# Half 1's output product of a two-branch decoder layer in seven products in place of eight

## The chip, the cores and the metric

The kernel runs on one core of a Trainium2 chip. The metric is the device time of one execution in microseconds (us), the median of the runs. One execution was also profiled; the rows of its trace are quoted below. Engines: TensorE (PE, with its weight loads as PEld), VectorE (DVE), ScalarE (ACT), GpSimd (POOL) and SyncE (SP), which issues nearly all DMAs, in order.

## The reference, cut to what matters

```python
xn = rms_norm(h, norm_gain[l])
proj = xn @ w_in[l]                       # queries, keys, values, gates of both branches
...                                       # o_sb: stick-breaking attention, o_sw: sliding window
y_sb = (o_sb * jax.nn.silu(sb_z)) @ w_branch_sb[l]
y_sw = (o_sw * jax.nn.silu(sw_z)) @ w_branch_swa[l]
merged = jax.nn.sigmoid(g_sb) * y_sb + jax.nn.sigmoid(g_sw) * y_sw
h = h + merged @ w_out[l]
return rms_norm(h, final_norm_gain)[:, BLOCK:]
```

There are 2048 tokens of width 1024, in float32; `w_out` is 1024 x 1024. The change concerns `merged @ w_out`, the residual sum and the last norm, for half of the tokens.

## The kernel before, in words

Tokens are cut into four groups of 512 (`GT`), and the groups into two halves of two groups; half 0 holds groups 2 and 3, half 1 groups 0 and 1. Every float32 operand of a matmul is split into a high part and a low part (`A.copy` into the high tile, then `V.tensor_tensor(..., op=ALU.subtract)` for the low one), and a product of two operands is three matmuls: high x high, high x low, low x high. All of it is bound to an order of PE that is written out by hand (`tc.manual_schedule` for the PE engine over the whole kernel). In some stretches the orders of DVE and ACT are written by hand too, and there they run in the order of the program; elsewhere a scheduler that plans with modelled times chooses the order of DVE, ACT and of SP's DMAs. An engine works its own list in order: what waits holds all that is behind it.

The stages that matter, in order of time:

1. *Half 1's gate pairs* (`gate_pairs`, L1643, called at L1910). Eight gate columns are computed in four pairs, each by seven products of half the depth (`HK` = 4 tiles) in place of eight. The sums of weights are made in `pair_weights`, one pair ahead. The argument `along` is a generator that is advanced once per pair (L1688); for half 1 it is empty. Products take the PSUM tags g, z and t in turn, two banks each. Sums out of PSUM are made by `add` (L1661), and results go to DRAM through SP (`gate_out`, L1667, L1670). The tag `xs` (`ring_x`, four tiles of 256 KB) stands idle for most of this stage.

2. *Attention* of both kinds, and in its last stretch the operands for half 0's branch products.

3. `finish` (L426) runs for half 0, then for half 1: first the sliding-window branch by seven products (`branch_by_pairs`, L328), then the stick-breaking branch (L734 to L756): for each of 8 column tiles d and 2 groups g, 12 matmuls (`project`, L449 to L451), a gate multiplication out of PSUM (L744), a sum with the other branch (L746), and the split of `merged[d, g]` (L748, L751). The output weights of the first column half are loaded and split in the same loop (`out_weights`, L601 to L611).

4. *The output product* (L758 to L809): for each group, for each token tile t of 128 rows and each column half `ch` of 512, 24 matmuls (8 depth tiles by 3) into one bank, then a DVE sum with the x row (L802), an ACT square with a row sum (L809), and after both column halves the norm (`normed`, L764, with `rsqrt`, L130) and a DMA of the rows to `out`. After the first row tile the second column half of the output weights is loaded and split (L811). In half 1 the last row tile's second column half is computed in two pieces of 256 columns, so that the closing chain (L835 to L845) starts earlier.

Half 1's output product is the last stage of the kernel; its last matmul starts at 2054.84 us of a span of 2061.5 us. DVE and ACT are in hand-written order through half 1's branch products, up to the end of the first two row tiles of the output product (`hand.close()`, L824).

The lines are those of the profile:

Of the kernel before, what the change touches and what calls it, by code (L numbers as in the profile page):

```python
# [7 lines left out]
F32 = mybir.dt.float32  # L8
# [36 lines left out]
def f32(ap):  # L45
    return ap.bitcast(F32)
# [3 lines left out]
def tile_kernel(ctx, tc, x, xt, meta, metat, gain, w_in, w_sb, w_sw, w_out, sinks, fgain,  # L50
# [201 lines left out]
    def columns(t):  # L252
        return t.rearrange("p a b c -> p (a b c)")
# [169 lines left out]
            rest = lambda d=b + 1, z=zb, w=w[1]: close(d, z, w)  # L423
        return rest

    def finish(ringl, blk, away, blocks, ahead):  # L426
# [4 lines left out]
        def bank():  # L431
            return ps("gzt"[next(banks) % 3])
# [4 lines left out]
        def small(tag, bufs):  # L437
            return cp.tile([P, GT], F32, tag=tag, name=tag, bufs=bufs)
# [32 lines left out]
        def next_half(ga, gb):  # L471
# [120 lines left out]
            yield  # L592
            yield

        gen = [blocks]
        outputs_left, last_x = [], [None]
        hand = ExitStack()
        for half, groups in enumerate(halves):
            part, merged, wo = {}, {}, {}

            def out_weights(k, ch, later=None):  # L601
                raw = small("a", AB)
                loaded[0] = DMA(raw, w_out[0, k * P:(k + 1) * P, ch * GT:(ch + 1) * GT]).ins
                ring = ringl if k < ((0, 2), (1, 3))[half][ch] else ringr
                h, l = wo[k, ch] = ring(), ring()
                A.copy(h, raw)
                low_part = lambda: V.tensor_tensor(l, raw, f32(h), op=ALU.subtract)
# [120 lines left out]
            before(14)  # L728
            if half == 0:
                DMA(fg, fgain.to_broadcast([P, D]))  # L730
            for d in range(2):
                out_weights(d, 0)
            ws_of = {}
            for d, g in [(d, g) for ds in ([0, 1], *([d] for d in range(2, 8))) for g in groups for d in ds]:  # L734
# [9 lines left out]
                V.tensor_tensor(gt, acc, gt, op=ALU.mult)  # L744
                t = part[d, g]
                V.tensor_tensor(t, gt, t, op=ALU.add)  # L746
                mh, ml = merged[d, g] = ringl(), ringl()
                A.copy(mh, t)  # L748
                for f in after:
                    f()  # L750
                after[:] = [lambda ml=ml, t=t, mh=mh: V.tensor_tensor(ml, t, f32(mh), op=ALU.subtract)]  # L751
                if g == groups[1] and d < 6:
                    out_weights(d + 2, 0, after)
            for f in after:
                f()
            del after[:]  # L756
            side = next_half(*halves[1]) if half == 0 else iter(())
            for g in groups:  # L758
                for t0 in range(0, 4, 2):
                    res, ssq, scaled_by = {}, {}, {}  # L760
# [13 lines left out]
                                V.scalar_tensor_tensor(res[t][:, cs], res[t][:, cs], rs[:, n:n + 1], fg[:, cs], op0=ALU.mult, op1=ALU.mult)  # L774
                            DMA(out[row:row + P, :], res[t])

                    end = (half, g, t0) == (1, groups[1], 2)
                    final = (half, g, t0) == (0, groups[1], 2)
                    paired = (g, t0) in ((groups[0], 0), (groups[1], 2))
                    order = [(n, t) for n in range(2) for t in (t0, t0 + 1)]  # L780
                    for ch, t in order if paired else sorted(order, key=lambda o: o[1]):
                        cs = slice(ch * GT, (ch + 1) * GT)
                        row = g * GT + t * P
                        if ch == 0:
                            res[t] = cp.tile([P, D], F32, tag="xr", name="res", bufs=3)
                            last_x[0] = DMA(res[t], x[row:row + P, :]).ins
                        ts = slice(t * P, (t + 1) * P)
                        last = end and t == 3
                        if ch == 0:
                            ssq[t] = pair[:, t - t0]  # L790
                        sum_of = ssq[t][:, ch:ch + 1]
                        if last:
                            rf = scaled_by[ch] = small("a", AB)
                        for i, c in enumerate((slice(0, GT // 2), slice(GT // 2, GT)) if last and ch else (slice(0, GT),)):
                            acc = bank()[:, :c.stop - c.start]
                            for k in range(KT):
                                (mh, ml), (wh, wl) = merged[k, g], wo[k, ch]
                                T.matmul(acc, lhsT=mh[:, ts], rhs=wh[:, c], start=k == 0, stop=False)
                                T.matmul(acc, lhsT=mh[:, ts], rhs=wl[:, c], start=False, stop=False)
                                T.matmul(acc, lhsT=ml[:, ts], rhs=wh[:, c], start=False, stop=k == KT - 1)  # L800
                            r = res[t][:, cs][:, c]
                            V.tensor_tensor(r, acc, r, op=ALU.add)  # L802
                            if last:
                                V.tensor_tensor(rf[:, c], r, fg[:, cs][:, c], op=ALU.mult)
                            if i:
                                s2 = cp.tile([P, 1], F32, tag="rs", name="rs2", bufs=4)
                                V.tensor_scalar(s2, sum_of, 1.0 / D, s0, op0=ALU.mult, op1=ALU.add)
                                s0, sum_of = s2, cp.tile([P, 2], F32, tag="ssq", name="ssq2", bufs=4)[:, 0:1]
                            A.activation(acc, r, AF.Square, accum_out=sum_of)  # L809
# [3 lines left out]
                        if (end or final) and ch and t == t0:  # L813
# [5 lines left out]
                        if last:  # L819
                            if ch == 0:  # L820
                                s0 = cp.tile([P, 1], F32, tag="rs", name="rs2", bufs=4)
                                V.tensor_scalar(s0, ssq[t][:, 0:1], 1.0 / D, EPS, op0=ALU.mult, op1=ALU.add)
                    if half and (g, t0) == (groups[0], 0):
                        hand.close()  # L824
                    if final:
                        outputs_left.append(lambda f=normed, t=t0: f(t + 1))
                    elif not end and paired:
                        normed(t0, t0 + 1)
                        next(side, None)
                    for t in (t0, t0 + 1):  # L830
                        row = g * GT + t * P
                        if end and t == 3:
                            s1 = sum_of
                            rs, u = (cp.tile([P, 1], F32, tag="rs", name="rs2", bufs=4) for _ in range(2))
                            A.activation(rs, s1, AF.Ln, bias=s0, scale=1.0 / D)  # L835
                            A.activation(rs, rs, AF.Exp, scale=-0.5)
                            V.tensor_scalar(u, s1, 1.0 / D, s0, op0=ALU.mult, op1=ALU.add)
                            V.scalar_tensor_tensor(u, rs, rs, u, op0=ALU.mult, op1=ALU.mult)
                            V.tensor_scalar(u, u, -0.5, 1.5, op0=ALU.mult, op1=ALU.add)
                            a, b = scaled_by[0], scaled_by[1]  # L840
                            A.activation(a, a, AF.Copy, scale=rs)
                            V.tensor_scalar(b, b, rs, u, op0=ALU.mult, op1=ALU.mult)
                            DMA(out[row:row + P, GT:], b)
                            A.activation(a, a, AF.Copy, scale=u)
                            A.dma_start(out[row:row + P, :GT], a)  # L845

    fst = ExitStack()
    xp = fst.enter_context(tc.tile_pool(name="x", bufs=1, side="right"))
# [778 lines left out]
    def sums_ahead(gs_, rs, short):  # L1627
# [12 lines left out]
            V.tensor_tensor(t[:, 4 * n:4 * n + 4], ssq[:, 0], ssq[:, 1], op=ALU.add)  # L1640
        rsqrt(rs, t, tp, t=u)

    def gate_pairs(ga, gb, pairs, pool, sums_x, nxt, ordered, along, between):  # L1643

        t1, t2, t3, t4 = sums_x[:4]
# [233 lines left out]
    for half, groups in enumerate(halves):  # L1879
        gts = [lambda spec=spec: gate(*spec) for spec in specs[half]]  # L1880
        if half == 1:
            with tc.tile_pool(name="fast1", bufs=1, side="left") as bp:
# [24 lines left out]
                        V.tensor_tensor(l, t, f32(h), op=ALU.subtract)  # L1907
                    byhand.close()
                hand.close()
                gate_pairs(*groups, pairs, bp, sums_x, nxt, rest, iter(()), lambda: None)  # L1910
            mid.close()
        with tc.tile_pool(name=f"swa{half}", bufs=1, side="left") as sp:
            m = half == 0
# [136 lines left out]
            A.preload_act_table_set("natural_log_exp_and_others")  # L2050
            byhand.close()
    fst.close()
    finish(ringl, blk, away, blocks[0], ahead)
    cst.close()

_OUT = (2048, 1024)
# [45 lines left out]
```

## Time and profile before

| | us |
|---|---|
| median of 3 runs | 2061.75 (2061.37 to 2062.23) |
| the profiled execution | 2063.17 |
| its span in the trace | 2061.5 |
| PE busy, of the span | 2043.9 |
| DVE busy, of the span | 1606.2 |
| ACT busy, of the span | 1160.7 |
| half 1's output product, first matmul to the tail | 1967.60 to 2055 |
| the tail, from there to the end | 6.5 |

How to read it: the span is the profiled execution from its first to its last instruction; the execution's own time is 1.7 us longer. Times in the rows are in us from the start of the span, L12 is line 12 of the kernel, and a row of the order of time has the start, the duration, the engine, the line and operation, output <- inputs, partitions x elements, and in brackets how long the engine stood idle before it and for what. Matmuls are pipelined: a row's duration overlaps the next, and what one costs is the distance between two starts.

### The profile page before, as it was taken

What the parts mean: (1) busy time and instruction counts of PE and PEld (TensorE: products, weight loads), DVE (VectorE), ACT (ScalarE), POOL (GpSimd) and SP (SyncE); (2) the same over time, 40 slices, a digit from 0 to 9 for tenths busy, and PEclk for the clock granted to TensorE, in tenths of its full rate; (3) what the DMA queues carried; (4) which work ended last, traced back from release to release, by engine and by line L of the source; (5) the groups of instructions that cost most, each with busy time, mean ns of one, the idle gap of its engine ahead of it and who ended that gap; (6) DMA issues with size and microseconds to landing.
All of it is one profiled execution on the core that took longest, in us unless ns stands there. A gap on an engine that the chain in (4) does not pass through costs nothing.

```text
span 2061.5 us, 31117 instructions
## 1 busy us (share of the span) xinstructions
PE 2043.9 (99%) x10435; PEld 1715.8 (83%) x10435; DVE 1606.2 (78%) x2639; ACT 1160.7 (56%) x2794; POOL 313.5 (15%) x642
## 2 busy tenths in 40 slices
PE   9999999999999999999999999999999999999998
PEld 7888888888888888888888888888888888887887
DVE  7898986877778787558787299999997688778843
ACT  6677775577655343357777366667765442234222
POOL 2233444431000000003332100000110003000000
PEclk9999999999999999999999999999999999999999
DMA  9855554765478566545444643333334679876822
GB/s 333 322 192 202 186 189 171 251 203 169 124 253 301 215 225 235 197 149 179 139 168 145 200 143 108 120 111 121 106 103 139 255 239 330 279 272 208 277 85 77
DMA packets 176144, 397.77 MB, mean 193 GB/s; under 512 B 24400, under 2 KB 28880, under 8 KB 175984
## 3 DMA queue, kind: packets, MB, share of 16 engines
q1 hardware_dynamic: 175696, 395.52, 56.9%
q8 instruction: 82, 1.34, 0.3%
q14 instruction: 78, 0.64, 0.1%
q10 hardware_dynamic: 288, 0.27, 0.0%
HBM read 249.02 MB, written 144.13 MB: 191 GB/s over the span
## 4 chain that ended last, share of the span: by engine, by line
PE 87%; DVE 5%; DMA 3%; ACT 3%; issue 1%; SPq 1%; POOL 0%; DVEq 0%; ACTq 0%
PE ps_g L931 34%; PE ps_o L1443 6%; PE ps_z L1386 6%; PE ps_t L1411 6%; PE ps_z L1227 3%; PE ps_o L1283 2%; PE ps_z L931 2%; PE ps_t L1261 1%; PE ps_g L1655 1%; PE ps_g L1656 1%; PE ps_g L1657 1%; PE ps_z L1655 1%; PE ps_z L1656 1%; PE ps_z L1657 1%; PE ps_o L337 1%; PE ps_t L1655 1%
## 5 line engine op out<-in xcount | busy, mean ns | idle before, releaser
L931 PE MATMUL ps_g<-xh,wh 128*128 128x512 f32 x1088 | 442.5, 407 | 0.7 <-ACT xh L1726 0.5
L931 PE MATMUL ps_g<-xl,wh 128*128 128x512 f32 x1088 | 426.3, 392 | 0.7 <-DVE xl L1727 0.6
L931 PE MATMUL ps_g<-xh,wl 128*128 128x512 f32 x1088 | 425.8, 391 | 0.0
L1396 DVE TENSOR_TENSOR_SCAN row<-row 128x512 f32<-128x512 f32 (+4 forms) x256 | 289.0, 1129 | 35.6 <-POOL row L1391 17.8
L931 PEld LDWEIGHTS ps_g<-xh,wl 128*128 128x128 f32 x1088 | 204.3, 188 | 45.1
L1389 ACT ACTIVATE row<-ps_z 128x512 f32<-128x512 f32 (+4 forms) x352 | 175.2, 509 | 110.2 <-PE ps_z L1386 106.9
L931 PEld LDWEIGHTS ps_g<-xl,wh 128*128 128x128 f32 x1088 | 205.4, 189 | 34.5 <-DVE xl L1727 2.0
L931 PEld LDWEIGHTS ps_g<-xh,wh 128*128 128x128 f32 x1088 | 205.0, 188 | 34.6 <-ACT xh L1726 1.5
L128 DVE SCALAR_TENSOR_TENSOR wtl<-ps_t,wth 128x512 fp32r<-128x512 f32 (+1 forms) x320 | 188.5, 589 | 11.3 <-ACT wth L127 11.1
L127 ACT ACTIVATE wth<-ps_t 128x512 fp32r<-128x512 f32 (+1 forms) x320 | 171.6, 536 | 43.9 <-PE ps_t L1411 40.1
L1386 PE MATMUL ps_z<-kt,q 128*128 128x512 f32 (+4 forms) x704 | 184.2, 350 | 0.7 <-ACT row L1389 0.7
L1411 PE MATMUL ps_t<-ident,row 128*128 128x128 f32 x1088 | 172.5, 274 | 3.4 <-DVE wtl L128 3.2
L1411 PEld LDWEIGHTS ps_t<-ident,row 128*128 128x128 f32 x1088 | 132.9, 140 | 38.3 <-DVE wtl L128 8.8
L1386 PEld LDWEIGHTS ps_z<-kt,q 128*128 128x128 f32 x704 | 123.8, 188 | 24.1 <-ACT row L1389 3.1
L1443 PE MATMUL ps_o<-wth,vc 128*128 128x512 f32 (+1 forms) x320 | 135.0, 422 | 0.0
L1443 PE MATMUL ps_o<-wtl,vc 128*128 128x512 f32 (+1 forms) x320 | 116.6, 364 | 0.2 <-DVE wtl L128 0.2
L1235 ACT ACTIVATE sc<-sc,nm 128x129 f32<-128x129 f32 x256 | 100.0, 393 | 29.6 <-DVE nm L1233 28.7
L1402 POOL COPY mr<-row 128x16 f32<-128x16 f32 x128 | 32.8, 258 | 385.0 <-DVE row L1396 349.8
L1220 POOL COPY sc<-skb 128x4 f32<-128x4 f32 x64 | 17.2, 276 | 459.2 <-PE ps_g L1657 304.9
L1394 DVE TENSOR_TENSOR_SCAN row<-row,mask 128x512 f32<-128x512 f32 (+2 forms) x64 | 69.8, 1098 | 16.9 <-ACT row L1389 16.8
L1082 ACT ACTIVATE tmp<-ps_g 128x512 f32<-128x512 f32 x63 | 37.8, 600 | 77.1 <-PE ps_g L931 71.3
L1267 POOL TENSOR_SCALAR_AFFINE_SELECT pm<-ph 64x256 fp32r<-64x256 f32 x128 | 63.4, 496 | 111.9 <-ACT ph L127 107.7
(679 smaller groups left out, 4651.4 us busy)
## 6 DMA issues: line engine op xcount, KB each, us to landing
wh<-h_in_w_in SPq DMA_DIRECT2D x66, 512.0 KB, 3.9
wl<-l_in_w_in SPq DMA_DIRECT2D x66, 512.0 KB, 5.1
raw<-in_w_in SPq DMA_DIRECT2D x57, 512.0 KB, 5.4
h_in_w_in<-wh SPq DMA_DIRECT2D x50, 512.0 KB, 3.1
l_in_w_in<-wl SPq DMA_DIRECT2D x50, 512.0 KB, 4.1
q<-qd SPq DMA_DIRECT2D x128, 128.0 KB, 3.1
vc<-vd SPq DMA_DIRECT2D x48, 256.0 KB, 3.2
kd<-tmp SPq DMA_DIRECT2D x32, 256.0 KB, 3.1
```

The costliest lines, as they stand in the source:

```text
L127: A.activation(h, acc, AF.Copy, scale=scale)
L128: V.scalar_tensor_tensor(l, acc, scale, f32(h), op0=ALU.mult, op1=ALU.subtract)
L931: T.matmul(acc, lhsT=a[:, k, :], rhs=b[:, k, :], start=k == i == 0, stop=k == KT - 1 and i == 2)
L1235: A.activation(sc[:, hh, :], sc[:, hh, :], AF.Exp, bias=nm[:, hh:hh + 1], accum_out=den[:, hh:hh + 1])
L1267: G.affine_select(out=pm[to, :, c], in_=full[r, :, c], pattern=[[0, 4], [sign, HB]], compare_op=ALU.is_ge, fill=0.0, base=n - 1, channel_m ...
L1386: T.matmul(z[:, :m], lhsT=qt[:, j * P:(j + 1) * P], rhs=kt[h][:, k0 + c:k0 + c + m], start=t == 0, stop=t == 1)
L1389: A.activation(r[:, c:c + m], z[:, :m], AF.Sigmoid, scale=-1.0)
L1394: V.tensor_tensor_scan(r[:, :w], r[:, :w], mask[:, :w], 1.0, op0=ALU.mult, op1=ALU.max)
L1396: V.tensor_tensor_scan(r[:, :w], r[:, :w], r[:, :w], last[j] if n else 1.0, op0=ALU.mult, op1=ALU.min)
L1411: T.transpose(tr[:, j * P:(j + 1) * P], rows_of[h, g, n - (j > i), j][:, k0:k0 + P], ident)
L1443: T.matmul(o[:, :n], lhsT=v, rhs=r, start=first and r is wh, stop=last)
L1655: T.matmul(acc, lhsT=wh[:, k, :], rhs=h[:, k, :], start=k == 0, stop=False)
```

## The change

Write merged (transposed) of half 1 as blocks by depth half and token group, and `w_out` as blocks by depth half and column half. The product of the two 2 x 2 block matrices is made by seven block products in place of eight: two token groups by two column halves. One block product has four token tiles, each of 4 depth tiles x 3 matmuls = 12 matmuls.

- `output_weight_sums` (new) is the generator that `gate_pairs` of half 1 gets as `along`. Per pair it loads four 128 x 512 tiles of `w_out`, makes four DVE sums of them in place and stores them in DRAM under the names t1 to t4.
- In `finish`, half 1's stick-breaking loop takes the column tiles in the order 0, 4, 1, 5, 2, 6, 3, 7, loads the output weights of the first column half in the order 4 to 7, 0 to 3, puts the split parts into tiles that the branch products have left (`dead`), and splits `merged` of the second group only for d >= 4. At (6, first group) it asks for four x row tiles, after the loop for the other eight pieces.
- `by_quads` (new) makes the output product. A list `todo` of 52 items (a sum or a low part on DVE, most with a copy on ACT) is worked off three at a time behind each row (`work()`). The sums of the output weights come back from DRAM (`fetched`) into tiles whose last product is over. The seven products are: second block of the first group by weight block 21; first by 11; s1 by t1; s2 by t2; s4 by block 22; s3 by t3; block 22 by t4. The products with s2, s3 and t4 accumulate in the banks of the second product (tags o and t), the one with s4 in those of the third (tags g and z). Rows are normed one behind the other (`norm`, `normed`); rows of the second group are scaled in part by ACT. The last row of the last product is computed in two pieces of 256 columns.
- The loop at L758 serves half 0 alone. DVE and ACT stay in hand-written order to the end.

The diff, cut to its core:

```diff
+        def by_quads(ga, gb, raws, a11, a12, a22, b11, b21, res, gone):
...
+            c11, c12, c21, c22 = ([raws[d, g] for d in ds] for ds, g in (
+                (range(HK), ga), (range(HK, KT), ga), (range(HK), gb), (range(HK, KT), gb)))
...
+            own("s1", osb_tiles)
+            fetched("t1", osb_tiles, weight_sums("t1"))
+            own("s2", extra)
...
+            todo = [summed(c22[k], c21[k], c22[k], ALU.add, ("s1", k)) for k in ks]
+            todo += [low_of("s1", k, c22[k], "t1") for k in ks]
+            todo += [summed(c21[k], c11[k], c21[k], ALU.subtract) for k in ks]
+            todo += [low_there("t1", k) for k in ks]
+            todo += [summed(c11[k], c22[k], c11[k], ALU.subtract, ("s2", k)) for k in ks]
+            todo += [low_of("s2", k, c11[k], "t2") for k in ks]
+            todo += [low_there("t2", k) for k in ks]
+            todo += [summed(c12[k], c12[k], c11[k], ALU.subtract, ("s4", k)) for k in ks]
+            todo += [both(low_of("s4", k, c12[k]), lambda k=k: A.copy(places["b22"][k][0], c22[k])) for k in ks]
+            todo += [low_of("b22", k, c22[k]) for k in ks]
...
+            todo += [s3_low(k) for k in ks]
+            todo += [low_there("t3", k, "t4") for k in ks]
+            todo += [low_there("t4", k) for k in ks]
+
+            def work(n=3):
+                for f in todo[:n]:
+                    f()
+                del todo[:n]
+
+            zs_ = [ps("o"), ps("t"), ps("o"), ps("t")]
+            xs_ = [ps("g"), ps("z"), ps("g"), ps("z")]
+
+            def product(acc, a, b, t, start=False, stop=False, c=slice(0, GT)):
+                ts = slice(t * P, (t + 1) * P)
+                for k in range(HK):
+                    (ah, al), (bh, bl) = a[k], b[k]
+                    T.matmul(acc[:, c], lhsT=ah[:, ts], rhs=bh[:, c], start=start and k == 0, stop=False, skip_group_check=True)
+                    T.matmul(acc[:, c], lhsT=ah[:, ts], rhs=bl[:, c], start=False, stop=False, skip_group_check=True)
+                    T.matmul(acc[:, c], lhsT=al[:, ts], rhs=bh[:, c], start=False, stop=stop and k == HK - 1, skip_group_check=True)
...
+            for t in rows:
+                product(xs_[t], a12, b21, t, True, True)
+                add(ga, t, 0, xs_[t])
+                work()
+            again = lend(*a12, *b21)
+            fetched("t2", again, weight_sums("t2"))
+            own("b22", again)
+            for t in rows:
+                product(zs_[t], a11, b11, t, True)
+                add(ga, t, 0, zs_[t])
+                work()
...
+            for k in ks:
+                DMA(c22[k], w_out[0, (k + HK) * P:(k + HK + 1) * P, GT:])
+            fetched("t3", again, weight_sums("t3"))
+            for t in rows:
+                product(xs_[t], places["s1"], places["t1"], t, True)
+                add(gb, t, 1, xs_[t])
+                work()
+            own("s3", lend(*places["s1"]))
+            fetched("t4", lend(*places["t1"]), weight_sums("t4"))
+            for t in rows:
+                product(zs_[t], places["s2"], places["t2"], t)
+                add(ga, t, 1, zs_[t])
+                work()
+            lag = []
+            for t in rows:
+                product(xs_[t], places["s4"], places["b22"], t, stop=True)
+                add(ga, t, 1, xs_[t])
+                square(ga, t, 1)
+                work()
+                lag = normed(lag, ga, t)
...
+            def seventh(t, lag):
+                product(zs_[t], places["s3"], places["t3"], t)
+                add(gb, t, 1, zs_[t])
+                square(gb, t, 1)
+                lag = normed(lag)
...
+            def fourth(t, lag):
+                product(zs_[t], a22, places["t4"], t, stop=True)
+                add(gb, t, 0, zs_[t])
+                square(gb, t, 0)
+                V.tensor_tensor(c12[t], res[gb, t][0], fg[:, :GT], op=ALU.mult)
+                return normed(lag, gb, t)
+
+            lag = seventh(0, lag)
+            lag = seventh(1, lag)
+            for t in range(3):
+                lag = fourth(t, lag)
+                if t < 2:
+                    lag = seventh(t + 2, lag)
...
+            for acc, c in zip(xs_, parts):
+                product(acc, a22, places["t4"], t, True, True, c)
+                V.tensor_tensor(r[:, c], acc[:, c], r[:, c], op=ALU.add)
+                A.activation(waste[:, c], r[:, c], AF.Square, accum_out=sum_of)
+                if c is parts[0]:
+                    normed(lag)
...
+            for c in parts:
+                V.tensor_tensor(rf[0][:, c], r[:, c], fg[:, c], op=ALU.mult)
...
+    def output_weight_sums():
+
+        for k in range(HK):
+            b11, b12, b22, b21 = (ring_x() for _ in range(4))
+            for t, (kk, ch) in ((b11, (k, 0)), (b12, (k, 1)), (b22, (k + HK, 1)), (b21, (k + HK, 0))):
+                DMA(t, w_out[0, kk * P:(kk + 1) * P, ch * GT:(ch + 1) * GT])
+            V.tensor_tensor(b11, b12, b11, op=ALU.subtract)
+            V.tensor_tensor(b12, b22, b12, op=ALU.subtract)
+            V.tensor_tensor(b22, b22, b11, op=ALU.subtract)
+            V.tensor_tensor(b21, b21, b22, op=ALU.subtract)
+            for name, t in (("t1", b11), ("t2", b22), ("t3", b12), ("t4", b21)):
+                out_sums[name, k] = dram(f"o{name}{k}", [P, GT])
+                DMA(out_sums[name, k], t)
+            yield
...
-                gate_pairs(*groups, pairs, bp, sums_x, nxt, rest, iter(()), lambda: None)
+                gate_pairs(*groups, pairs, bp, sums_x, nxt, rest, output_weight_sums(), lambda: None)
```

More of the change, by code (lines that the diff above doesn't have):

```diff
@@ L730, in finish @@
                 DMA(fg, fgain.to_broadcast([P, D]))
[L731 to L734, printed above, removed]
+            if half:
+                names = "t2", "b22", "t3", "t4"
+                first = [columns(vm[:, 2:4]), columns(vm[:, 0:2]), wm[1], wm[0]]
+                dead = iter([*(t for name in names for k in range(HK) for t in blk[name, k]), *(ringl() for _ in range(4))])
+                fresh = lambda: next(dead)
+                order, turn = (0, 4, 1, 5, 2, 6, 3, 7), [(4 + j) % 8 for j in range(8)]
+            else:
+                order = turn = range(8)
+            turn = iter(turn)
+            for _ in range(2):
+                out_weights(next(turn), 0)
+            ws_of, raws, res = {}, {}, {}
+            for d, g in [(d, g) for ds in (order[:2], *([d] for d in order[2:])) for g in groups for d in ds]:
                 if d not in ws_of:
@@ L756, in finish @@
             del after[:]
-            side = next_half(*halves[1]) if half == 0 else iter(())
+            if half:
+                u = columns2(wp.tile([P, KT, P], F32, tag="raw", name="raw", bufs=2))
+                res[gb, 0] = u[:, :GT], u[:, GT:]
+                for i in range(1, 4):
+                    res[gb, i] = small("a", AB), small("a", AB)
+                for i in range(4):
+                    row = gb * GT + i * P
+                    for ch in (1, 0):
+                        DMA(res[gb, i][ch], x[row:row + P, ch * GT:(ch + 1) * GT])
+                by_quads(ga, gb, raws, *([merged[d, g] for d in ds] for ds, g in (
+                    (range(HK), ga), (range(HK, KT), ga), (range(HK, KT), gb))),
+                    [wo[k, 0] for k in range(HK)], [wo[k, 0] for k in range(HK, KT)], res,
+                    [osb[k, g] for g in groups for k in range(4)])
+                hand.close()
+                return
+            side = next_half(*halves[1])
             for g in groups:
@@ L787, in finish @@
                         ts = slice(t * P, (t + 1) * P)
-                        last = end and t == 3
                         if ch == 0:
                             ssq[t] = pair[:, t - t0]
[L791 to L809, printed above, removed]
+                        acc = bank()
+                        for k in range(KT):
+                            (mh, ml), (wh, wl) = merged[k, g], wo[k, ch]
+                            T.matmul(acc, lhsT=mh[:, ts], rhs=wh, start=k == 0, stop=False)
+                            T.matmul(acc, lhsT=mh[:, ts], rhs=wl, start=False, stop=False)
+                            T.matmul(acc, lhsT=ml[:, ts], rhs=wh, start=False, stop=k == KT - 1)
+                        r = res[t][:, cs]
+                        V.tensor_tensor(r, acc, r, op=ALU.add)
+                        A.activation(acc, r, AF.Square, accum_out=ssq[t][:, ch:ch + 1])
                         if (g, t, ch) == (groups[0], 0, 0):
@@ L812, in finish @@
                                 out_weights(k, 1)
-                        if (end or final) and ch and t == t0:
+                        if final and ch and t == t0:
                             normed(t)
@@ L818, in finish @@
                             normed(t)
[L819 to L824, printed above, removed]
                     if final:
                         outputs_left.append(lambda f=normed, t=t0: f(t + 1))
-                    elif not end and paired:
+                    elif paired:
                         normed(t0, t0 + 1)
                         next(side, None)
[L830 to L845, printed above, removed]
     fst = ExitStack()
```

169 lines of the change are left out of this document (159 added, 10 removed).

## The prediction

> **What bounds the kernel now.** I read the page first, then the busy times of the stretches that the change touches, then the order of time inside them. The first two lines say that TensorE (PE) is busy for 99% of the span.
>
> ```profile
> span 2061.5 us, 31117 instructions
> PE 2043.9 (99%) x10435; PEld 1715.8 (83%) x10435; DVE 1606.2 (78%) x2639; ACT 1160.7 (56%) x2794; POOL 313.5 (15%) x642
> ```
>
> The second view is the table of stretches. The first four rows cover half 1's four gate pairs, the fifth the stick-breaking branch product of half 1, the sixth its output product, the last the tail. Columns: from and to, length, busy us (x instructions) of PE, weight loads, DVE, ACT, POOL, then granted clock, DMA share, GB/s.
>
> ```profile
> 775.00:795.00 20.00, 20.00 (x90) 16.57 (x89) 15.66 (x26) 6.38 (x12) 0.00 (x0) 1.00 0.65 236
> 795.00:815.00 20.00, 20.00 (x90) 16.55 (x89) 13.04 (x22) 5.90 (x10) 0.00 (x0) 1.00 0.83 294
> 815.00:835.00 20.00, 20.00 (x90) 16.58 (x89) 12.93 (x22) 5.43 (x10) 0.00 (x0) 1.00 0.63 221
> 835.00:855.00 20.00, 20.00 (x90) 16.57 (x89) 8.77 (x15) 4.19 (x7) 0.00 (x0) 1.00 0.48 164
> ...
> 1921.36:1967.60 46.24, 46.24 (x205) 38.30 (x204) 37.98 (x58) 14.21 (x24) 0.00 (x0) 1.00 0.77 253
> 1967.60:2055.00 87.40, 87.40 (x409) 73.29 (x407) 35.09 (x82) 18.78 (x53) 0.00 (x0) 1.00 0.21 73
> 2055.00:2061.50 6.50, 0.12 (x1) 0.00 (x0) 2.00 (x7) 2.45 (x6) 0.00 (x0) 0.82 0.42 161
> ```
>
> PE never rests in the first six, at clock 1.00; so each matmul taken out pays in full, as long as no new wait appears. In the output product DVE is busy for 35 of 87 us, so there is room to put sums beside PE. What one matmul costs is its distance to the next (busy times overlap):
>
> ```profile
> 1967.60 0.39 PE L798 MATMUL ps_z<-ringl 128*128 128x512 f32 x1
> ...
> 2049.20 0.28 PE L798 MATMUL ps_z<-ringl 128*128 128x256 f32 x1
> ...
> 2052.08 0.28 PE L798 MATMUL ps_t<-ringl 128*128 128x256 f32 x1
> ...
> 2054.84 0.28 PE L800 MATMUL ps_t<-ringr,ringl 128*128 128x256 f32 x1
> ```
>
> The stage starts at 1967.60. Fifteen of its sixteen groups, 15 x 24 = 360 matmuls of 512 columns, end at 2049.20: 81.60 / 360 = 0.2267 us each. The sixteenth runs as two halves of 256 columns; 24 matmuls take 2.88 us, 0.120 each.
>
> **What is removed.** Before: 360 x 0.2267 + 48 x 0.120 = 87.4 us, the measured stretch. After, each of seven products has four rows of 12 matmuls; the last row runs in halves: 27 x 12 x 0.2267 + 24 x 0.120 = 73.4 + 2.9 = 76.3 us. That is **-11.0 us**. Removed too are eight loads, eight ACT copies and eight DVE low parts of the second column half's output weights; they lay beside a full PE, so I count nothing.
>
> The Trainium skill, "TensorE: Matmul & The Clock Gate", section "Part 1", gives a warm spacing of about 215.7 ns at 512 columns; by that the 48 removed rows of work would be 10.4 instead of 10.9 us, but the 226.7 ns of this trace decide.
>
> **What is added in the last stage.** Call the first product's start 0 (1967.60 now). One row of a product lasts 12 x 0.2267 = 2.72 us, a product 10.88. Behind each of the first rows DVE has one sum out of PSUM and three queued sums or low parts; there are 52 of the latter. Prices:
>
> ```profile
> 1967.80 0.69 DVE L744 TENSOR_TENSOR gt<-ps_g,gt 128x512 f32<-128x512 f32 x1 [0.70 <-PE ps_g L451]
> 1968.53 0.69 DVE L746 TENSOR_TENSOR ringl<-gt,ringl 128x512 f32<-128x512 f32 x1
> 1969.14 1.52 DVE L751 TENSOR_TENSOR ringl<-ringl 128x512 fp32r<-128x512 f32 x2
> ...
> 1977.05 1.89 DVE L607 TENSOR_TENSOR ringr<-a,ringr 128x512 fp32r<-128x512 f32 x3
> ...
> 2049.40 0.69 DVE L802 TENSOR_TENSOR res<-ps_g,res 128x512 f32<-128x512 f32 x1 [3.81 <-PE ps_g L800]
> 2050.13 0.60 ACT L809 ACTIVATE ps_g<-res 128x512 f32<-128x512 f32 x1 [4.72 <-DVE res L802]
> 2050.67 0.19 ACT L809 ACTIVATION_READ_ACCUMULATOR ps_g<-res 128x1 f32 x1
> 2050.89 0.16 DVE L767 TENSOR_TENSOR ssq<-ssq 128x1 f32<-128x1 f32 x1 [0.79 <-ACT ps_g L809]
> 2051.08 0.15 DVE L132 TENSOR_SCALAR ssq<-ssq 128x1 f32<-128x1 f32 x1
> 2051.33 0.20 ACT L133 ACTIVATE rs<-ssq 128x1 f32<-128x1 f32 x1 [0.47 <-DVE ssq L132]
> 2051.56 0.20 ACT L134 ACTIVATE rs<-rs 128x1 f32<-128x1 f32 x1
> ...
> 2053.60 1.42 DVE L774 SCALAR_TENSOR_TENSOR res<-res,rs,fg 128x512 f32<-128x512 f32 x2
> ```
>
> Three low parts in 1.89 us: one each 0.60. A PSUM sum 0.69, begun 0.20 after the next PE row starts (2049.40 against 2049.20). So a row costs DVE 0.69 + 3 x 0.60 = 2.5 us, less than 2.72: it keeps up. Deadlines: the third product (21.8 us) needs queue items 0 to 15, done behind row 6: 6 x 2.72 + 0.2 + 2.5 = 19.0. The fourth (32.6) needs 28, behind row 10: 29.9. The fifth (43.5) needs 40, behind row 14: 40.8. The sixth (54.4) needs 48, behind row 16: 46.2. The least slack is 2.7 us; at 0.73 per item (1967.80 to 1968.53, a sum that needs the one just before it) a row would be 2.9 us, 0.2 late per row, 2.5 us at row 14: still just covered. ACT's two copies a row hide easily beside its 0.8 us square. Cost **0**, with 3 us if the cover is gone.
>
> The loads are asked for a product ahead. The hardest is t1: its slots come free at 0, eight x loads (2 MB) stand before it in SP's queue, it must have landed for the low parts behind row 5 (13.6 us).
>
> ```profile
> a<-in_w_out SPq DMA_DIRECT2D x15, 256.0 KB, 4.3
> ...
> res<-in_x SPq DMA_DIRECT2D x5, 512.0 KB, 3.6
> ```
>
> 3 MB at the 294 / 0.83 = 354 GB/s that the second stretch implies take 8.9 us: in time. The loads of t2, t3, t4 and of the second weight quarter wait on SP for tiles that PE or DVE is still reading; behind them stand only each other and the outputs. Cost 0.
>
> Three small things do reach PE or the end. First, the first row's last matmul uses the low part of merged (7, first group), which stands behind two DVE sums of the last branch tile: now begun at 1969.14, done at 1969.83, 2.23 us into the stage; needed at 11 x 0.2267 = 2.49. I take **+0.1**. Second, in the fifth product the norm of the row before falls due as well: sum 0.69, small ones 3 x 0.2, two at 0.19, two of 1.42 / 2 = 0.7, with a wait of 0.2 for the square (1.49 us from the sum's start to 2050.89): 3.3 us a row and 3.7 where one queued item is left, against 2.72. From row 17 to 20 DVE falls 2.2 us behind, so the sum of the next row starts at 59.5, not 57.3, and ends at 60.2, while the last product's first row, which accumulates into that bank, could start at 54.4 + 5.4 = 59.8: **+0.4**. Third, the last row's halves are now 12 x 0.120 = 1.44 us apart, not 2.88, and row 2's norm must pass DVE between them. Its square is ready 1.7 us after the final row starts, two small steps end at 2.1, the first half's sum at 2.5, ACT's two steps at 2.6, three small ones 3.3, one scaling 4.0; PE ends at 3.0, so the last sum starts 0.8 late: **+0.8**. The closing chain differs by two more half-wide multiplications on DVE; ACT's path is the longer one now:
>
> ```profile
> 2055.15 0.42 DVE L802 TENSOR_TENSOR res<-ps_t,res 128x256 f32<-128x256 f32 x1
> ...
> 2056.72 0.22 DVE L838 SCALAR_TENSOR_TENSOR rs<-rs,rs 128x1 f32<-128x1 f32 x1 [0.35 <-ACT rs L836]
> ...
> 2057.47 0.72 ACT L844 ACTIVATE a<-a,rs 128x512 f32<-128x512 f32 x1
> ```
>
> Two multiplications and two small steps after the sum (about 1.2 us from its end, plus 0.2) push L838's step from 1.15 to some 1.45 us; L844 then finds its factor just when it is free: **+0.1**.
>
> **What is added in the gate pairs.** Per pair: four loads of 256 KB, four DVE sums (2.4 us), four stores. DVE has 20 - 15.7 = 4.3 us or more free in each of the four stretches. DMA: 2.1 MB in 20 us are 105 GB/s, against 354 - 294 = 60 free in the fullest stretch and 118 or more in the others; a transfer is late there by 45 x 20 / 354 = 2.5 us. The weights that it can delay are asked for far ahead:
>
> ```profile
> 803.61 0.32 SPq L60 DMA_DIRECT2D wh<-h_in_w_in  x1
> ...
> L1655 PE MATMUL ps_g<-xh,wh x4: 389/389/390, 820.0 to 822.0; 128*128 128x512 f32 x4
> ```
>
> The load goes out at 803.61, for a pair whose second product starts at 820.0 and its first 2.7 us earlier: 13 us of cover. Bounds: below, 0 (nothing on PE is removed there); above, all sixteen sums exposed, 16 x 0.6 = 9.6. I take **0**, nearest to the row with 13.04 of 20 us.
>
> Sum: -11.0 + 0.1 + 0.4 + 0.8 + 0.1 = **-9.6 us**. The profiled execution took 2063.17 us around its span of 2061.5; it would become 2053.6. From the median of 2061.75 I forecast **2052.2 us**.
>
> **Rivals.** (A) *Operands come late in the last stage.* For it: 2.7 us of slack is one row, and DVE enters the stage with its own waits:
>
> ```profile
> DVE gt L744 <- DMA gt<-gs: 1.4, 1, 1.4
> ```
>
> A branch gate came 1.4 us late once; the x loads now share that queue. A DVE that starts 3 to 6 us late delays the first or third product by 2 to 5: 2054 to 2057.6. Against: PE does not wait once there now. Chance 0.20.
>
> (B) *DVE is held in the gate pairs by the new loads.* DVE works in order; a sum whose load has not landed holds the sums that free PSUM. The bank to watch is that of the fifth product:
>
> ```profile
> L1655 PE MATMUL ps_z<-xh,sh x4: 388/389/390, 806.4 to 808.4; 128*128 128x512 f32 x4
> ...
> 800.93 0.69 DVE L1661 TENSOR_TENSOR tmp<-ps_z,tmp 128x512 f32<-128x512 f32 x1
> ...
> SPq L60 <- DVE tmp L1667: 35.3, 11, 6.1
> ```
>
> It is freed at 801.6 and written again at 806.4: cover 4.8 us. A hold of h us in each pair costs 4 x (h - 4.8). From h = 6.2 less than 4.1 us of the gain is left; from h = 4.8 + (9.6 + 4.1) / 4 = 8.2 the kernel is slower. A load behind SP's longest wait here (6.1) that lands in 4.3 gives h = 10.4: +22.4 - 9.6, or 2074.6. For it: SP did wait 35.3 us on DVE results in 760 to 900 us. Against: half the buffers are idle long before, and the loads wait for nothing else. Chance 0.12 within the bound, 0.07 slower.
>
> By the Trainium skill, "DMA: Bandwidth & Descriptors", section "Specifications", a core gets about 358 GB/s of HBM; 294 + 105 = 399 would exceed that and speak for (B).
>
> ```profile
> GB/s 311 284 399 393 248 7 297 319 366 184 135 261 412 416 163 361 0 117 83 107 350 376 347 305 173 18 117 260 330 109 117 146 268 60 198 389 354 113 47 381
> ```
>
> The slices of 780 to 870 us reach 416 GB/s with one core at work, so the trace does not show that limit.
>
> (C) *The eighth product isn't gone*, because the split last row or zero work fills it: the diff counts 348 matmuls against 408. Chance 0.01, 2062 us.
>
> **Chances.** My forecast, 2050.0 to 2054, 0.60; (A) 0.20; together faster, 0.80. Within 0.2% (4.1 us, about what a measurement of this kernel can tell from no change) 0.13, slower 0.07. The range reaches from 2050.0 (all 11.0 us kept, and 0.7 for the spread of the runs) to 2057.6, the end of (A): 0.80.
>
> **What would show it.** PE instructions 10435 - 60 = 10375; an output stage of about 77 us; PE idle there under 1 us, at the last product's first row; the four gate stretches with PE still 20.00 of 20.00 and DVE 2.4 us a pair higher; the end some 7.6 us after the last matmul's start, which is 6.7 now (2054.84 to 2061.5). A PE wait on a DVE sum or low part at 0, 22, 33 or 44 us of the stage is (A). A PE wait between 780 and 860 us is (B). The forecast is wrong where DVE needs more than 2.7 us a row, or where the new order moves a wait into an earlier stage.

## The result, and the profile after

The changed kernel took **2049.53 us** (median of 4 runs, 2049.44 to 2049.86) beside 2061.56 us for the kernel before (4 runs, 2059.80 to 2062.23): a ratio of 0.9943, 95% interval 0.9926 to 0.9960. It is faster by 12.0 us, where 9.6 had been forecast, and lies 0.5 us under the low end of the range. The profiled execution after took 2049.44 us around a span of 2047.7.

The first lines of the page after: 60 matmuls fewer, as counted, so rival (C) falls; and 11.6 us less of PE's busy time.

```profile
span 2047.7 us, 31246 instructions
PE 2032.3 (99%) x10375; PEld 1706.0 (83%) x10375; DVE 1648.4 (80%) x2708; ACT 1178.4 (58%) x2825; POOL 312.4 (15%) x642
```

The table of stretches after, columns as in the prediction: four of the gate pairs, the stick-breaking branch product, the output product, the tail.

```profile
775.00:795.00 20.00, 20.00 (x90) 16.54 (x90) 15.74 (x26) 6.93 (x14) 0.00 (x0) 1.00 0.73 251
795.00:815.00 20.00, 20.00 (x90) 16.58 (x89) 16.99 (x29) 6.01 (x10) 0.00 (x0) 1.00 0.91 330
815.00:835.00 20.00, 20.00 (x90) 16.57 (x89) 16.48 (x27) 5.94 (x10) 0.00 (x0) 1.00 1.04 403
835.00:855.00 20.00, 20.00 (x90) 16.58 (x89) 11.91 (x18) 3.70 (x7) 0.56 (x4) 1.00 0.88 319
1917.65:1963.89 46.24, 46.24 (x205) 38.29 (x204) 35.29 (x54) 11.73 (x20) 0.00 (x0) 1.00 0.78 258
1963.89:2040.25 76.36, 76.36 (x349) 63.63 (x347) 67.86 (x134) 36.88 (x87) 0.00 (x0) 1.00 0.33 108
2040.25:2047.70 7.45, 0.12 (x1) 0.00 (x0) 3.32 (x12) 3.22 (x8) 0.00 (x0) 0.65 0.38 141
```

Read it against the seven rows of before. PE is busy for every microsecond of the gate pairs, though DVE rose from 50.4 to 61.1 us in the four rows together and the DMAs from 294 to 403 GB/s in the fullest. The output product went from 87.40 to 76.36 us without one gap on PE: **-11.04**. The tail went from 6.50 to 7.45: **+0.95**. Stage and tail together gave 10.1 us. The two profiled spans differ by 13.8, so 3.7 us came from work ahead of the stage that the change doesn't touch: the output product starts at 1963.89 in place of 1967.60.

Matmul by matmul the lead grows to 0.4 us at 65 us of the span, 2.0 at 1661 and 3.7 from 1863 on. The largest part of it, 1.7, thus arises in half 1's sliding-window branch. There PE's waits are the following; columns: us in all, times, longest. Before:

```profile
PE ps_g L337 <- ACT ringl L343: 1.4, 1, 1.4
PE ps_o L338 <- DVE ringl L458: 0.7, 1, 0.7
```

After:

```profile
PE ps_o L338 <- DVE ringl L458: 0.7, 1, 0.7
PE ps_g L337 <- ACT ringl L343: 0.4, 1, 0.4
```

The same wait at the same line is 1.0 us shorter, and the instructions of DVE, ACT and SP stand in the same order there in both kernels. So one of two things holds. Theory V: these waits differ from run to run, whatever the kernel. Theory S: the sums of the output weights, which run far ahead of this point, shift something that helps here. The experiments start with that.

### The profile page after: what moved, and what is told of

It reads as the page before. It is cut to its first block, busy times and chain, and to the rows that moved or that the text cites. A ratio compares the mean times of both kernels' runs of the same rounds, so it can differ in the third digit from the quotient of the medians.

```text
span 2047.7 us, 31246 instructions
## 1 busy us (share of the span) xinstructions
PE 2032.3 (99%) x10375; PEld 1706.0 (83%) x10375; DVE 1648.4 (80%) x2708; ACT 1178.4 (58%) x2825; POOL 312.4 (15%) x642
## 4 chain that ended last, share of the span: by engine, by line
PE 88%; DVE 4%; DMA 4%; ACT 2%; SPq 1%; issue 1%; POOL 0%; DVEq 0%; ACTq 0%
PE ps_g L1188 34%; PE ps_o L1700 6%; PE ps_z L1643 6%; PE ps_t L1668 6%; PE ps_z L1188 3%; PE ps_z L1484 3%; PE ps_o L1540 2%; PE ps_t L1518 1%; PE ps_o L338 1%; PE ps_o L337 1%; PE ps_o L339 1%; PE ps_g L1929 1%; PE ps_g L1930 1%; PE ps_g L1931 1%; PE ps_z L1929 1%; PE ps_z L1931 1%
```

## The experiments

The kernel before was measured again beside each group of them: 2060.07 us (median of 21 runs, 2058.25 to 2062.35) beside the first four experiments, 2060.21 (20 runs) beside the next four, 2060.26 (12 runs) beside the last two.

**Both kernels once more.** No edit.

> The kernel before, unchanged, for a second profile. The changed kernel gained 12.0 us of median, though its output stage alone gained 10.1 us (11.0 fewer in matmuls, 0.95 more in the tail); the rest, 2 us of median and 3.7 us of the two profiles, arose ahead of that stage. Theory V (the waits ahead of it vary from run to run with when DMAs land): median 2060 to 2062, ratio 1.000, and the PE gaps in half 0's and half 1's branch stages add up to something other than the 3.0 us of the first profile, by at least 0.5 us. Theory S (the changed kernel's new DMAs and order do away with those waits): median 2061.5, and the same 3.0 us of gaps at the same matmuls.

> The changed kernel, unchanged, for a second profile. Both theories: median 2049.5, no PE gap in the output stage. Theory V: the start of the output stage lies up to 1 us from 1963.9. Theory S: within 0.3 us of it, and the same single waits of 0.5 and 0.8 us in half 1's branch stage.

Measured: before 2060.32 us (11 runs, 2058.80 to 2063.66), ratio 1.0003 [0.9994, 1.0012]; after 2049.91 us (5 runs, 2048.74 to 2051.04), ratio 0.9949 [0.9937, 0.9962]. In the kernel before, PE's waits in the sliding-window branches of both halves (L337 and L338) came to 2.8 us in the first profile and to 1.7 in the second. The stretch of sixty matmuls in half 1's sliding-window branch is the telling one. Columns as above; the changed kernel in its first profile:

```profile
1851.54:1866.81 15.27, 14.24 (x61) 11.11 (x60) 14.98 (x25) 11.11 (x22) 0.00 (x0) 1.00 0.71 247
```

The same program in its second profile:

```profile
1851.55:1868.37 16.82, 14.77 (x62) 10.95 (x60) 15.38 (x26) 12.22 (x24) 0.00 (x0) 1.00 0.73 259
```

Up to its start the two executions are 0.01 us apart; the same matmuls then take 15.27 us once and 16.82 once, 1.55 us more. What DVE and PE wait for, in the first profile of after (DVE first, from the view of 1820 to 1870 us):

```profile
DVE a L307 <- DMA a<-in_w_sw: 1.2, 1, 1.2
...
DVE a L497 <- DMA nt<-a: 0.4, 1, 0.4
```

and in the second:

```profile
DVE a L497 <- DMA nt<-a: 1.4, 1, 1.4
...
DVE a L307 <- DMA a<-in_w_sw: 1.1, 1, 1.1
```

```profile
PE ps_g L337 <- ACT ringl L343: 1.4, 1, 1.4
```

DVE waited 1.0 us longer for one DMA (L497). It was 0.6 us later in the second profile even before that: the same sum out of PSUM starts at 1814.55 us in the first and at 1815.18 in the second. At 1846 us DVE is 1.6 us late, and that is what PE loses: 1.0 in the wait shown, the rest in small steps ahead of it. The kernel before differs likewise between its two profiles: its stretch took 16.86 us once and 15.86 once. So within each kernel the stretch varies by 1.0 to 1.6 us, as much as between the two kernels, and V accounts for the size. The output stage of the changed kernel starts at 1965.48 us in its second profile, 1.6 us later than in its first, more than the 1 us that V had set. That the DMA makes 1.0 us of it is read from the traces, not tried; where DVE's other 0.6 us come from stays open.

**The sums alone, and the product without them.** The first adds the new generator to the kernel before, which doesn't use what it stores; the second takes it out of the kernel after and loads other stored tiles of the same size, so that its output is another one.

```diff
-                gate_pairs(*groups, pairs, bp, sums_x, nxt, rest, iter(()), lambda: None)
+                gate_pairs(*groups, pairs, bp, sums_x, nxt, rest, output_weight_sums(), lambda: None)
```

```diff
-                return [out_sums[name, k] for k in range(HK)]
+                kk, g = {"t1": (0, ga), "t2": (HK, gb), "t3": (0, gb), "t4": (HK, ga)}[name]
+                return [zw[k + kk][g] for k in range(HK)]
...
-                gate_pairs(*groups, pairs, bp, sums_x, nxt, rest, output_weight_sums(), lambda: None)
+                gate_pairs(*groups, pairs, bp, sums_x, nxt, rest, iter(()), lambda: None)
```

> The kernel before, with the output weights' sums made and stored in half 1's gate pairs and used by nobody. My step priced them at 0, with 9.6 us as the upper end. Theory V: 2060 to 2062, ratio 1.000. Theory S: 2059.5, since the new DMAs alone would do away with 2 us of waits later. If the sums cost something on PE: above 2063, with PE gaps between 780 and 860 us.

> The changed kernel without the sums of output weights: the four loads per product bring stored gates of the same shape in their place, so the output is another. Theory V: 2049.5 within 0.7 us. Theory S: 2051.5, as the waits ahead of the stage come back. If the sums cost time where they stand: below 2048.5.

Measured: 2059.41 us (11 runs), ratio 0.9995 [0.9987, 1.0004], for the sums alone; 2049.59 us (5 runs), ratio 0.9948 [0.9936, 0.9961], for the product without them. The first number is the one that was set for S, but the kernel before, too, came out lower than expected, at 2060.07 us. The sums alone lie 0.7 us under it, with an interval from 2.7 us under to 0.8 over, where S asked for 2 under: this run doesn't decide. The other does: without the sums the changed kernel lies 0.3 us under the same kernel with them (2049.91), where S asked for 2 above. S falls in its full size; that the sums bring some tenths of a microsecond is not excluded. A cost of theirs above 0.8 us is excluded, and rival (B) falls: PE waits for nothing between 770 and 870 us, neither in this kernel nor in the changed one. The kernel with the sums alone, in the fullest of the gate stretches:

```profile
815.00:835.00 20.00, 20.00 (x90) 16.57 (x89) 14.53 (x24) 6.09 (x11) 0.00 (x0) 1.00 1.04 406
```

406 GB/s, and PE is still busy for 20.00 of 20.00.

**The eighth product put back.** In the first product:

```diff
+                product(xs_[t], a12, b21, t, True, True)
                 product(xs_[t], a12, b21, t, True, True)
```

> The kernel after, with its first output product computed twice (48 more matmuls of 128x512; the second pass restarts the banks, so nothing else changes). Theory P (PE is full in this stage, so the whole gain is the work of the eighth product): PE never idle in the stage, the stage 48 x 0.2267 = 10.9 us longer, the kernel 1.0 to 1.7 us above the kernel before (its tail is 1.0 longer): about 2060.5. Rival Q (some of the gain came from elsewhere, the gate pairs or fewer loads): at least 2 us below that, 2058 or less.

Measured: 2061.30 us (11 runs), ratio 1.0007 [0.9997, 1.0016], 1.1 us above the kernel before, as P had set. The output product of this kernel:

```profile
1962.66:2049.89 87.23, 87.23 (x397) 72.64 (x395) 67.95 (x134) 36.88 (x87) 0.00 (x0) 1.00 0.27 94
```

87.23 - 76.36 = 10.87 us for 48 matmuls, 0.2265 each, and no gap. The gain of the stage is the eighth product's PE time and nothing else (P).

**More work for DVE.** How near was the forecast's bound of 2.72 us a row?

```diff
             def work(n=3):
+                V.tensor_tensor(spent, fg[:, :GT], fg[:, GT:], op=ALU.add)
                 for f in todo[:n]:
```

> The kernel after, with one more sum of 128x512 on VectorE (0.6 us, its result unused) behind each row of the first five products. My row model: VectorE then needs 0.69 + 4 x 0.60 = 3.1 us a row against 2.72, falls 0.37 behind per row, and TensorE waits first at the fourth product (about 1.3 us), about 2.8 us in all by the fifth: the kernel after plus 2.8 (1.3 to 4). Rival: VectorE has much more room than the model says, because the operands are due later than their rows: no wait, within 0.5 us of the kernel after.

Measured: 2057.62 us (11 runs), 7.7 us above the kernel after, where 2.8 had been expected: a miss. PE's longest wait in this kernel, and the rows of PE around it:

```profile
PE ps_o L701 <- DVE rs L730: 5.6, 1, 5.6
```

```profile
2024.47 0.39 PE L703 MATMUL ps_t<-ringl,ringr 128*128 128x512 f32 x1
2030.47 0.77 PE L701 MATMUL ps_o<-ringl,ringr 128*128 128x512 f32 x1 [5.61 <-DVE rs L730]
2031.03 0.63 PE L702 MATMUL ps_o<-ringl,ringr 128*128 128x512 f32 x1
2031.45 0.63 PE L703 MATMUL ps_o<-ringl,ringr 128*128 128x512 f32 x1
```

The stretch of that wait, and the one behind it:

```profile
2024.70:2030.47 5.77, 0.16 (x2) 0.03 (x1) 5.61 (x16) 1.65 (x7) 0.00 (x0) 0.73 0.35 129
2030.47:2034.34 3.87, 3.87 (x9) 3.10 (x10) 3.62 (x7) 1.33 (x4) 0.00 (x0) 0.52 0.60 219
```

The place of the wait was wrong: no operand is late. For the third to the fifth product the prediction had asked that all three queued items of the row be done before the product starts; but only the first of the three is due, and it is read late. The fifth product's last low part starts on DVE at 2008.07 us and is first read at 2010.64, 2.3 us into that product. All the lag comes due at one point, the last product's first row, which needs the bank that DVE has not yet read; in the prediction that was the term of +0.4. DVE's sums were 3.01 us apart through the first sixteen rows (1967.78 to 2015.89 us), 0.29 a row behind PE, plus the lag of the norms. And the price was wrong: behind the wait of 5.6 us the granted clock is 0.52, and nine matmuls stand 0.43 us apart in place of 0.227, another 1.8 us. The Trainium skill, "TensorE: Matmul & The Clock Gate", section "Part 1", says that the clock drops to half after an idle window of about 3.4 us and comes back after as long a busy one, with 426.7 ns between matmuls of 512 columns meanwhile. This trace agrees on the spacing and on the way back: 3.87 us at 0.52, 0.43 us apart. The drop came sooner here: the granted clock is 1.00 from 2024.70 to 2027.35 us and 0.50 from 2027.40 on, some 2.5 us behind PE's last work.

**Half of that work.** The added sum behind the last ten rows only:

```diff
+                if len(todo) <= 22:
+                    V.tensor_tensor(spent, fg[:, :GT], fg[:, GT:], op=ALU.add)
```

> The kernel after, with the extra VectorE sum of 128x512 behind the last ten of the twenty rows only. Seen with twenty: rows 3.01 us apart on VectorE against TensorE's 2.72, the eighth group of sums 6.2 us later than without, 0.56 us of it covered, one TensorE wait of 5.6 us at the last product's first row, and then nine matmuls 0.43 apart (half clock) in place of 0.227. If VectorE's lag simply adds up until that bank is needed: ten sums make it 6.2 - 10 x 0.29 = 3.3 us late, a wait of 2.8 us at the same place. If only a long rest halves the clock: no slow matmuls behind it and the kernel after plus 2.8 us, about 2052.7. If any rest does: plus 4.5 or more.

Measured: 2054.42 us (8 runs, 2052.68 to 2055.83), 4.5 us above the kernel after, the figure that was set for half clock behind any rest. The profiled execution is the lowest, 2052.68: 2.8 us above, the figure that was set for a wait without slow matmuls. Its one wait in this stage, and the rows of PE:

```profile
PE ps_o L702 <- DVE rs L731: 2.7, 1, 2.7
```

```profile
2023.73 0.39 PE L704 MATMUL ps_t<-ringl,ringr 128*128 128x512 f32 x1
2026.87 0.47 PE L702 MATMUL ps_o<-ringl,ringr 128*128 128x512 f32 x1 [2.74 <-DVE rs L731]
2027.17 0.40 PE L703 MATMUL ps_o<-ringl,ringr 128*128 128x512 f32 x1
2027.41 0.39 PE L704 MATMUL ps_o<-ringl,ringr 128*128 128x512 f32 x1
```

The wait has the place and the size that the adding up of the lag gives (2.8), and in this execution the granted clock stays at 1.00 through the wait and behind it: the first matmuls stand 0.30 and 0.24 us apart, and the stage is 3.0 us longer. The other seven runs are 0.8 to 3.2 us above it. Their mean clocks are 0.997 to 0.999 (0.999 in the profiled one), so some of them probably lost clock behind the same wait. A rest of 2.7 us would then halve the clock in some executions and not in others; without the traces of the others that stays open.

**The tail.** Three kernels for the term of +0.8. The first puts the last rows in another order and scales both halves of row 2 on ACT, the second has the order alone, the third ACT alone.

```diff
-                    if g == gb and (ch == 0 or t < 2):
+                    if g == gb:
...
-            for t in range(3):
-                lag = fourth(t, lag)
-                if t < 2:
-                    lag = seventh(t + 2, lag)
+            lag = fourth(0, lag)
+            lag = seventh(2, lag)
+            lag = fourth(1, lag)
+            lag = fourth(2, lag)
+            lag = seventh(3, lag)
```

> The kernel after, with the last rows put in another order, so that no row's norm falls between the two halves of the last row (row 2's comes one row earlier), and with both halves of row 2 scaled on ScalarE. If the last sum is late because of that norm (my term of +0.8): the time from the last matmul's start to the end falls from 7.6 to about 6.8 us and the kernel by 0.7. Rival: the closing chain is bounded by ScalarE and the last store, and the tail stays within 0.2 us of 7.6.

> As the run before in this list, but with the order of the rows alone; row 2's second half stays on VectorE. If it is the order that frees VectorE between the two halves: the same tail of about 6.8 us. If ScalarE taking over the scaling matters: a tail between 7.0 and 7.6.

> The kernel after in its own order of rows, with both halves of row 2 scaled on ScalarE. Together with the new order this took the tail from 7.6 to 6.8 us, the order alone 0.1. If VectorE's scaling between the two half sums was the whole delay: the same 6.8. If ScalarE then holds the last row's squares for one more scaling (0.7 us): 7.0 to 7.6, and both parts are needed.

Measured from the last matmul's start to the end: after 7.61 us; order and ACT 6.81; order alone 7.52; ACT alone 7.59. The medians: 2048.86, 2050.01 and 2050.55 us (5 runs each); ratios 0.9946 [0.9933, 0.9959], 0.9950 [0.9936, 0.9964], 0.9952 [0.9939, 0.9964]. DVE's rows in the kernel after, with the last matmul's start at 2040.09:

```profile
2039.34 0.42 DVE L819 TENSOR_TENSOR a<-ps_g,a 128x256 f32<-128x256 f32 x1
2039.93 0.22 DVE L727 SCALAR_TENSOR_TENSOR rs<-rs,ssq 128x1 f32<-128x1 f32 x1 [0.17 <-ACT rs L725]
2040.19 0.15 DVE L728 TENSOR_SCALAR rs<-rs 128x1 f32<-128x1 f32 x1
2040.37 0.16 DVE L729 TENSOR_TENSOR rs<-rs 128x1 f32<-128x1 f32 x1
2040.57 0.75 DVE L737 SCALAR_TENSOR_TENSOR a<-a,rs,fg 128x512 f32<-128x512 f32 x1
2041.24 0.42 DVE L819 TENSOR_TENSOR a<-ps_z,a 128x256 f32<-128x256 f32 x1
```

With order and ACT both changed, the last matmul starts at 2039.89:

```profile
2039.66 0.42 DVE L820 TENSOR_TENSOR a<-ps_g,a 128x256 f32<-128x256 f32 x1
2040.21 0.42 DVE L820 TENSOR_TENSOR a<-ps_z,a 128x256 f32<-128x256 f32 x1
```

The last sum starts 1.15 us after the last matmul's start in the first and 0.32 in the second: 0.83 us is what row 2's norm between the half sums cost, as forecast. The order alone leaves DVE's scaling ahead of the last sums: the last one starts 0.89 us after the last matmul's start. ACT alone frees that sum (0.37 us), but it gives ACT one more scaling ahead of the last square, which starts 1.72 us after the last matmul's start, where the kernel after had 1.60. Only both together free the end. This version is the best measured. Against the kernel after its gain is shown by the traces (0.8 us of tail), not by the medians, whose intervals overlap.

## Why the prediction was right and wrong

- *-11.0 for the matmuls*: right. 11.04 in the profile; 10.87 when put back.
- *0 for DVE's row of 2.5 us*: right. DVE waited 0.2 us for PE at each row from the second to the fifth product's first.
- *0 for the gate pairs*, and rival (B): the cost is 0 by two experiments. The load was as heavy as forecast, the cover sufficed.
- *+0.1 for the first row's last low part*: 0. It was done 2.23 us into the stage and due at 2.49, by the prediction's own figures; there was no reason to take anything.
- *+0.4 at the last product's first row*: 0. The place was right, as the two kernels with more DVE work show; the size was off. DVE fell 1.27 us behind, not 2.2, as these sums of after show, against PE's 2.72 a row:

```profile
2013.05 0.69 DVE L704 TENSOR_TENSOR res<-ps_z,res 128x512 f32<-128x512 f32 x1
2016.35 0.69 DVE L704 TENSOR_TENSOR res<-ps_g,res 128x512 f32<-128x512 f32 x1
2019.42 0.68 DVE L704 TENSOR_TENSOR raw<-ps_z,raw 128x512 f32<-128x512 f32 x1
2022.48 0.69 DVE L704 TENSOR_TENSOR raw<-ps_o,raw 128x512 f32<-128x512 f32 x1
```

  The rows took 3.30, 3.07 and 3.06 us, where 3.3 to 3.7 had been set. The last of these sums frees the bank at 59.2 us of the stage (58.59, plus the 0.60 at which sums follow each other), 0.6 ahead of need.
- *Rival (A)*: it did not occur. A branch gate did come late, and held DVE for 2.9 us once ahead of the stage (1.4 before), but DVE had caught up by the first row, whose sum started 2.93 us into the stage, where 2.92 had been set. PE waited for nothing in the stage.
- *+0.9 at the tail*: right, 0.95. The last sum was 0.83 us late where +0.8 had been set.

By steps the change is worth 11.04 - 0.95 = 10.1 us, and 10.2 by the medians of the repeated runs (2060.07 and 2049.91): ratio 0.9949, where 2052.2 / 2061.75 was 0.9954. **The step that failed is the base and its spread**: "From the median of 2061.75 I forecast 2052.2 us" and "0.7 for the spread of the runs". The median of three runs stood 1.5 to 1.7 us above the kernel's medians of 12 to 21 runs, and single runs of one kernel spread over 3 to 5 us, not 0.9. Of the 64 later runs of the kernel before, 14 lie as high as the three did (2061.37 or more); the fourth run of the result took 2059.80. So the three were a stroke of bad luck, or high for a reason that no run shows. The prediction had a hint at hand: the profiled execution took 2063.17 us, 0.9 above the highest of the three. Against the 2.7 us by which the forecast was high, the two waits that did not occur make 0.5; the rest is about the 1.5 to 1.7 us of the base and what the runs after scatter (2049.53 and 2049.91). From a base of 2060.2 us the same sum gives 2050.6, and a low end of 2048.5 (2060.2 - 11.0 - 0.7), which takes the measured time in. The mechanism of the prediction, the matmuls' time less a small tail, was right.

## What to carry to other kernels

On a full TensorE a matmul taken out is worth its spacing, to 0.1 us in 11; what has to be worked out is whether the operand work beside it keeps up, row by row, and the place to look at is the bank that is written again while its last reader lags. Price a queue by the distance between starts, not by durations, and check each wait that is taken against its own due time. And before a forecast in absolute time, ask how far single runs of the unchanged kernel lie apart: here that was more than all the small terms together.

## What was not expected of the hardware

- The same program, with the same order on each engine, took 15.27 and 16.82 us for one stretch of sixty matmuls; in the second DVE had waited 1.0 us longer for one DMA. Why that transfer lands late in some executions stays open.
- A wait of 2.7 us cost 3.0 in its profiled execution; one of 5.6 us cost 7.6, since the clock was halved for most of 3.9 us behind it. The drop came some 2.5 us after PE's last work in the one, and in the other 2.7 us of rest passed at full clock.
- One core's DMAs moved 403 to 406 GB/s over 20 us, with TensorE undisturbed.
